# Chunk 0 of a two-layer encoder trunk: the z products of two channel groups side by side on four accumulators, with u's folds and the token rows loaded behind them

## The chip, the cores and the metric

The kernel runs on one core of a Trainium2 chip. The metric is the device time of one execution in microseconds: the median of three runs. All matrix work is done on TensorE (PE in the profile); VectorE (DVE), ScalarE (ACT) and GpSimd (POOL) convert, evict and do the elementwise work; SyncE (SP) issues nearly all transfers.

## The reference, cut to what matters

The input is x with 2048 rows (tokens) of 1024 channels. Layer 0, around which the change turns:

```python
h = rms_norm(x, a_norm)                     # per row
u, z = jnp.split(h @ a_w_in, 2, axis=-1)    # 1024 columns each
# u: four groups of 256 channels; trailing means over 2, 4, 8, 16 rows, minus the row itself
pooled = stack(means) - u
mixed = einsum('bsgc,gcd->bsgd', pooled, w_group) * scale
x = x + (mixed * silu(z)) @ a_w_out
x = x + (p @ ple_w) * sigmoid(x @ ple_gate_w)
```

Layer 1 is a stick-breaking attention of 16 heads with shared keys and values, again with a SiLU gate, an output product and the gated embedding.

## The kernel before

The 2048 rows are cut into four chunks of 512. In the first part of the kernel each chunk runs through 22 steps in a list `steps`: eight z and u steps (four groups of 256 channels each), four output products (`run_o`), four gates with embedding (`run_g`), and six for q, k and v (`run_kvq`). The attention, with what is left of layer 1 as filler, is the second part.

**Products.** Each fp32 operand is split in a high and a low half in a 'round' format that TensorE takes at one pass, and a product is three passes: high times high, high times low, low times high. So `product` for 256 output channels runs over 8 slices of 128 input channels (kt), with 2 blocks x 3 passes = 6 matmuls of 128x128 against 512 rows each: 48 matmuls, into two accumulators in PSUM. Between the slices it takes one step of a generator `beside`, with which other work is written into TensorE's program. The row norm is multiplied in only when the sums are evicted, so that products can run before the norm is known.

**Folds.** The group maps (`grp`, 256x256) are applied to u's weights instead of u: in chunk 0 `fold(g)` takes the raw weights of u (`uraw`, from `wut`), splits them (four steps `across`, ACT L418 and DVE L419), multiplies them with the map (four steps `mapped`, 12 matmuls of 256 columns each, L429, here called a fold tile) and evicts each tile in halves on ACT (L436) and DVE (L437) with the norm's gain `g_a`. Chunks 1 to 3 reread the folded weights and z's split weights from DRAM, where `queue` has stored them.

**Chunk 0's start.** `load_first(3)` queues on SP the x tiles of chunk 0 (8 of 256 KB) and the raw z weights of group 3 (4 of 256 KB) in turns. Then come fold 3's raws, its map, two small tiles of gains, fold 2's raws and its map, and, from the loop over the steps, z2's raws. `prep(0)` splits the x tiles (L326, L327); `first_weights` splits the z weights with the gain (ACT L356, DVE L360). The order of the steps is z3, u3, z2, u2, z1, u1, z0, u0. In it:

- z3 runs beside `prep`'s last steps and the `across` steps of fold 3; `first_beside` writes the fold's tiles behind it. Then come the stores of z3's split weights (`settle`) and the loads of the four token tiles (`load_tokens`, 512 KB each). z3 stays in its accumulators.
- u3 runs beside fold 2 and the squares of the tokens (ACT L306). Behind it `bcast` turns the row factor (L249: four transposes) and spreads it to the tile `rb` (L254), and `gate_of` evicts z3 (DVE L511, sigmoid on ACT L512, GpSimd L513).
- z2 runs beside the `across` steps of fold 1 (`turning(1)`), u2 beside its tiles; z1 and u1 do the same for fold 0. After each u its pooling follows (L528 to L549, DVE and GpSimd).

**Order and buffers.** The program is put in its final order by a scheduler that works with costs of its own; `keep_in_program_order` (also as `stay`) pins an instruction among the pinned ones of its engine. SP's transfers of this part are pinned. PSUM has eight banks: four in `psd`, two in `psboth`, two in `pst`. `dense()` deals `psd` and `psboth` out, two to one; `turned()` gives `pst`. `pair()` gives one of 18 split tiles, the pools `wpair` and `wboth` hold 12 pairs of weights.

Of the kernel before, what the change touches and what calls it, by code (L numbers as in the profile page):

```python
# [15 lines left out]
P = 128  # L16
D = 1024
# [18 lines left out]
def trunk_kernel(ctx, tc, x, xt, pt0, wut, cols, heads, zin, grp, aout, agate, aple,  # L36
# [69 lines left out]
    class Weights:  # L106

        def __init__(self, src, kts, c0, n, gain=None, kept=None, stay=lambda ins: ins):
            self.src, self.c0, self.n, self.gain, self.kept, self.stay = src, c0, n, gain, kept, stay
            self.kk = min(W5 // n, kts)  # L110
            self.units, self.raws = [], {}
            self.k0s = list(range(0, kts, self.kk))
# [23 lines left out]
        def convert(self, half=0):  # L136
            kk, n, gain, kept, c0 = self.kk, self.n, self.gain, self.kept, self.c0
            self.reread()
            for k0 in self.part(half):
                if (kept, c0, k0) in split_once:  # L140
                    continue
                state["u"] += 1
                pr = wp[state["u"] % 2].tile([P, 2, kk, n], F32R, tag="wpair", name="wpair")
                self.units.append(pr)
                raw = self.raws.pop(k0)
                if gain is None:
                    self.stay(A.copy(out=pr[:, 0], in_=raw))  # L147
                    state["w"] += 1
                    self.stay((G if state["w"] % 3 else V).tensor_tensor(  # L149
                        out=pr[:, 1], in0=raw, in1=f(pr[:, 0]), op=ALU.subtract))  # L150
# [69 lines left out]
    with ExitStack() as st:  # L220
# [77 lines left out]
        def prep(s):  # L298
# [24 lines left out]
            for o in range(KT):  # L323
                low = (lambda: None) if s else first_weights(o)
                pr = pair("xp")
                stay(A.copy(out=pr[:, 0], in_=xs[o]) if s or o else V.tensor_copy(out=pr[:, 0], in_=xs[o]))  # L326
                stay(V.tensor_tensor(out=pr[:, 1], in0=xs[o], in1=f(pr[:, 0]), op=ALU.subtract))  # L327
# [7 lines left out]
        wz0 = {"raw": [], "pair": []}  # L335
# [12 lines left out]
        def first_weights(o):  # L348
            q, j = o // 2, o % 2
            raw, ga = wz0["raw"][q], g_a[:, o : o + 1]  # L350
            if not j:
                state["u"] += 1
                wz0["pair"].append(wp[state["u"] % 2].tile([P, 2, 2, 256], F32R, tag="wpair", name="wpair"))
            pr = wz0["pair"][q]
# [8 lines left out]
            def store():  # L363
                d = split_once["wi", wz0["c0"], 2 * q] = dram.tile([P, 2, 2, 256], F32, name=f"wz0_{q}")
                queue(out=d, in_=f(pr))
# [5 lines left out]
        def first_beside():  # L371

            raws, wg = chunk[0]["fold"].pop(3)
            lead, folded = prep(0), fold(3, raws, wg)
            next(lead)
            next(lead)

            def behind():
                for kt in range(KT):
                    next(lead, None)  # L380
                    for _ in range((0, 0, 0, 0, 0, 1, 1, 2)[kt]):
                        next(folded, None)
                    if kt == 6:
                        maps[3].convert()
                        wg.extend(maps[3].units)
                    yield
                next(folded, None)
                maps[2].convert()
                yield from folded

            return behind()

        def load_fold(g):
# [9 lines left out]
            if g < 3:  # L403
                maps[g] = Weights(grp[g], 2, 0, 256, stay=tc.keep_in_program_order)
# [3 lines left out]
        def fold(g, raws, wg):  # L408
# [13 lines left out]
            def mapped(i):  # L422
                ps = dense()
# [38 lines left out]
        def second_beside(g):  # L462
# [4 lines left out]
            for kt in range(KT):  # L467
                if g == 2 or kt > 3:
                    next(folded, None)
                if g == 2:  # L470
                    next(chunk[0]["squares"], None)
# [12 lines left out]
        def run_z(s, g, wz):  # L484
            ck = chunk[s]
            beside = ()
            if not s and g == 3:
                beside = first_beside()
                wz = wz0["pair"]
            elif not s and g:  # L490
                beside = turning(g - 1)
            elif s and g == 3:
                beside = row(s)
            pss2 = [dense(), dense()]
            product(pss2, wz, ck["x"], (0, P), range(KT), beside, by_term=not s and g == 3)
            settle()
            if not s and g == 3:
                for q in range(4):
                    load_tokens(0, q)
                ck["z3"] = pss2  # L500
                return
            if "rb" not in ck:
                ck["rb"] = bcast(ck["r"], "x")
# [13 lines left out]
        def run_u(s, g, wu):  # L517
# [3 lines left out]
            product(pss2, wu or ck["wu"].pop(g), ck["x"], (0, P), None, second_beside(g - 1) if g and not s else ())  # L521
            if "z3" in ck:
                ck["rb"] = bcast(ck["r"], "x")
                gate_of(ck, g, ck.pop("z3"))
# [296 lines left out]
        for s in range(NSUB):  # L821
            for g in (3, 2, 1, 0):
                def load(g=g, s=s, z=0):
# [4 lines left out]
                steps.append((lambda load=load: load(z=1), lambda *w, s=s, g=g: run_z(s, g, *w)))  # L828
                steps.append((load, lambda *w, s=s, g=g: run_u(s, g, *w)))
# [38 lines left out]
        maps = {3: Weights(grp[3], 2, 0, 256, stay=tc.keep_in_program_order)}  # L868
# [8 lines left out]
        ps = dense()  # L877
        for _ in range(10):
            T.matmul(ps[:, 0:P], ident, ident, start=True, stop=True)
# [7 lines left out]
        for i, (_, run) in enumerate(steps):  # L887
# [6 lines left out]
            if i in (1, 3):  # L894
                chunk[0]["fold"][1 - i // 2] = load_fold(1 - i // 2)
# [10 lines left out]
            elif i == 1:  # L906
                join_gains(wz0["gs"])
# [498 lines left out]
```

## Time and profile before

| | |
|---|---|
| median of three runs | 2639.67 us (2639.28 to 2640.36) |
| the profiled execution | 2641.07 us, span 2639.0 us |
| PE busy | 2628.7 us (100%) |
| DVE, ACT, POOL busy | 1991.9, 1422.6, 936.2 us |
| DMA, mean over the span | 228 GB/s |
| granted TensorE clock | 1.0 |
| chunk 0's z and u products | 5.54 to 121.92 us |

Times in the profile count from the start of the span. In a list of groups or in order of time, a row has start and duration in microseconds, the engine, the line of the kernel, the operation, the tile that it writes `<-` those that it reads, shapes, and a count after x; in brackets stands how long the engine had been idle and what ended that. `PEld` is the load of a matmul's stationary operand. In a table by stretch, a row has the stretch, its length, busy time with the count of instructions, the granted clock, the mean share of time that the DMA engines were busy, and GB/s. In a list of waits a row has who waited for whom, the sum in microseconds, the times and the longest.

### The profile page before, as it was taken

To read this page: it belongs to the slowest core of one execution; us is meant where nothing else is said; L and a number is where in the kernel's file an instruction comes from. 1 tells how busy PE (TensorE), PEld (TensorE's weight loads), DVE (VectorE), ACT (ScalarE), POOL (GpSimd) and SP (SyncE) were. 2 spreads that over 40 slices of the span, in tenths; PEclk is the share of its full clock that TensorE was granted. 3 is DMA by queue.
4 is the path that set the end of the run, shared out by engine and by line. 5 is a ranking of instruction groups with operands and counts; after the bars stand their busy time and mean duration, and the time that the engine had idled before them with its cause. 6 is when DMAs were issued, how large, how long until landed. Compare 5 with 4: busy or idle time off the path is not lost.

```text
span 2639.0 us, 38535 instructions
## 1 busy us (share of the span) xinstructions
PE 2628.7 (100%) x13046; PEld 2200.8 (83%) x13046; DVE 1991.9 (75%) x2583; ACT 1422.6 (54%) x2770; POOL 936.2 (35%) x740
## 2 busy tenths in 40 slices
PE   9999999999999999999999999999999999999999
PEld 7888888888888888888888888888888888888887
DVE  6877835677367763767599999999999998886642
ACT  5456623556136641355466666666666666665530
POOL 2664437644485444744221111122111211112320
PEclk9999999999999999999999999999999999999999
DMA  8648885588856878446787665656666777779875
GB/s 327 228 166 291 307 311 186 191 285 282 308 172 228 295 247 307 148 162 231 239 279 238 185 217 168 183 168 193 209 200 181 187 222 233 201 208 288 249 231 179
DMA packets 472994, 602.26 MB, mean 228 GB/s; under 512 B 29855, under 2 KB 309663, under 8 KB 472797
## 3 DMA queue, kind: packets, MB, share of 16 engines
q1 hardware_dynamic: 466008, 588.72, 67.9%
q0 software_dynamic: 4608, 8.39, 2.0%
q10 hardware_dynamic: 2180, 2.69, 0.4%
q8 instruction: 103, 1.69, 0.3%
q14 instruction: 95, 0.77, 0.1%
HBM read 440.24 MB, written 153.17 MB: 225 GB/s over the span
## 4 chain that ended last, share of the span: by engine, by line
PE 98%; DMA 1%; DVE 0%; ACT 0%; issue 0%; POOL 0%; SPq 0%; DVEq 0%; ACTq 0%
PE psd L176 27%; PE psd L658 20%; PE psa L1023 9%; PE psd L1085 6%; PE psd L1087 6%; PE psd L1089 6%; PE pso L1036 5%; PE psl L999 5%; PE pso L1035 5%; PE psl L998 5%; PE psdt L1085 1%; PE psdt L1087 1%; PE psdt L1089 1%; PE psd L429 1%; DMA xn<-in_x_dram 0%; DMA xin<-in_xt_dram 0%
## 5 line engine op out<-in xcount | busy, mean ns | idle before, releaser
L658 PE MATMUL psd<-wpair,x 128*128 128x512 f32 x2304 | 523.9, 390 | 0.0
L1010 DVE TENSOR_TENSOR_SCAN pp<-kap,pp,zeros 128x512 f32<-128x512 f32 x384 | 513.0, 1337 | 6.4 <-ACT kap L1002 5.5
L1026 ACT CAST at<-psa 128x512 fp32r<-128x512 f32 (+3 forms) x640 | 325.2, 523 | 345.9 <-PE psa L1023 334.5
L658 PEld LDWEIGHTS psd<-wpair,x 128*128 128x128 f32 x2304 | 432.3, 188 | 89.4
L1027 DVE TENSOR_TENSOR at<-psa,at 128x512 fp32r<-128x512 f32 (+3 forms) x640 | 374.8, 597 | 62.1 <-ACT at L1026 57.9
L1002 ACT ACTIVATE kap<-psl 128x512 f32<-128x512 f32 (+3 forms) x640 | 345.7, 540 | 90.0 <-PE psl L999 86.7
L176 PE MATMUL psd<-xp,wpair 128*128 128x512 f32 x1536 | 352.7, 390 | 1.0 <-DMA wpair<-wu 0.6
L176 PEld LDWEIGHTS psd<-xp,wpair 128*128 128x128 f32 x1536 | 287.2, 188 | 61.6 <-issue 1.0
L1023 PE MATMUL psa<-ident,pp 128*128 128x128 f32 x2176 | 328.8, 273 | 0.8 <-DVE at L1027 0.8
L1023 PEld LDWEIGHTS psa<-ident,pp 128*128 128x128 f32 x2176 | 264.0, 141 | 54.8 <-DVE at L1027 2.3
L998 PE MATMUL psl<-kk,qa 128*128 128x512 f32 (+3 forms) x640 | 275.4, 430 | 0.0
L1007 DVE TENSOR_TENSOR_SCAN pp<-kap,ahead 128x128 f32<-128x128 f32 (+3 forms) x256 | 226.0, 885 | 37.1 <-ACT kap L1002 35.7
L1036 PE MATMUL pso<-at,vv 128*128 128x512 f32 (+3 forms) x640 | 234.2, 366 | 0.0
L999 PE MATMUL psl<-kk,qb 128*128 128x512 f32 (+3 forms) x640 | 233.1, 364 | 0.0
L1035 PE MATMUL pso<-at,vv 128*128 128x512 f32 (+3 forms) x640 | 232.3, 363 | 0.0
L155 DVE SCALAR_TENSOR_TENSOR wpair<-wraw,gains,wpair 128x512 fp32r<-128x512 f32 x192 | 167.2, 891 | 58.2 <-ACT wpair L154 53.2
L176 PE MATMUL psd<-x,wpair 128*128 128x512 f32 x768 | 176.7, 389 | 0.0
L176 PE MATMUL psd<-mp,wpair 128*128 128x512 f32 x768 | 174.7, 389 | 0.0
L149 POOL TENSOR_TENSOR wpair<-wraw,wpair 128x512 fp32r<-128x512 f32 x99 | 144.1, 1464 | 76.7 <-ACT wpair L147 69.3
L176 PEld LDWEIGHTS psd<-x,wpair 128*128 128x128 f32 x768 | 144.2, 188 | 29.8
L176 PEld LDWEIGHTS psd<-mp,wpair 128*128 128x128 f32 x768 | 144.2, 188 | 29.9
L154 ACT ACTIVATE wpair<-wraw,gains 128x512 fp32r<-128x512 f32 x192 | 131.7, 717 | 59.5 <-DMA wraw<-in_bq_dram 30.0
(191 smaller groups left out, 4454.9 us busy)
## 6 DMA issues: line engine op xcount, KB each, us to landing
kk<-kd SPq DMA_DIRECT2D x160, 256.0 KB
vv<-vd SPq DMA_DIRECT2D x160, 256.0 KB
wraw<-in_kv_dram SPq DMA_DIRECT2D x128, 256.0 KB
wpair<-wzd SPq DMA_DIRECT2D x64, 512.0 KB
wpair<-wod SPq DMA_DIRECT2D x64, 512.0 KB
wpair<-wgd SPq DMA_DIRECT2D x64, 512.0 KB
wpair<-wu SPq DMA_DIRECT2D x48, 512.0 KB
wpair<-wi SPq DMA_DIRECT2D x36, 512.0 KB
```

What stands on the lines that cost most here:

```text
L176: T.matmul(ps, wst(units, kt, wh, c0), acts[kt][:, ah], start=(first and not wh and not ah), stop=(last and wh == 1))
L658: T.matmul(pss2[i], ck["x2"][kt][:, xh, tk], wst(ws, kt, wh, 0, W5), start=(kt == 0 and xh == 0 and wh == 0), stop=(kt == KT - 1 and wh == 1))
L998: T.matmul(ps[:, :w], qa[:, qs], kk[:, :w], start=True, stop=False)
L999: T.matmul(ps[:, :w], qb[:, qs], kk[:, :w], start=False, stop=True)
L1002: A.activation(out=kp[:, r0:], in_=ps[:, :w], func=AF.Sigmoid, scale=-1.0)
L1007: V.tensor_tensor_scan(out=pp[:, r0:][:, ::-1], data0=kp[:, r0:][:, ::-1], data1=ahead[:, r0:][:, ::-1], initial=1.0, op0=ALU.mult, op1=AL ...
L1010: V.tensor_tensor_scan(out=pp[:, ::-1], data0=kp[:, ::-1], data1=zeros.to_broadcast([P, W5]), initial=st["carry"][j], op0=ALU.mult, op1=AL ...
L1023: T.transpose(pt[:, j * P : (j + 1) * P], pp[:, r0 + kt * P : r0 + (kt + 1) * P], ident)
L1026: A.copy(out=at[:, 0, cs], in_=pt[:, cs])
L1027: V.tensor_tensor(out=at[:, 1, cs], in0=pt[:, cs], in1=f(at[:, 0, cs]), op=ALU.subtract)
L1035: T.matmul(po[:, cs], vv[:, kt, :], at[:, 0, cs], start=(st["diag"] and kt == 0), stop=False)
L1036: T.matmul(po[:, cs], vv[:, kt, :], at[:, 1, cs], start=False, stop=(st["last"] and kt == 3))
```

## The change

The first two steps of chunk 0 become one, `run_first`: z3 and z2 run quarter by quarter (two x tiles, then six matmuls a tile for group 3, and the same for group 2) on four accumulators, which take all of `psd`. `load_first` queues the raw weights of both groups between the x tiles; group 2's raws lie in the pool `tmp`. The token tiles are queued behind fold 3's raws and the gains, ahead of fold 2's raws; the stores of the split z weights (now eight) come behind all of these. The squares run within `run_first`, behind the last `across` steps of fold 3; then come one tile of fold 3, `bcast`, the gates of z3 and z2, fold 2's map, and the other three tiles. Fold 3's tiles use `psboth` and `pst`; the warm-up matmuls use `pst`. The maps' split pairs come from `pair()`. The steps then are u3 (beside fold 2), u2 (beside fold 1's `across`), z1 (beside its tiles), u1 (beside fold 0's `across`), z0 (beside its tiles), u0. `load_fold(1)` and `load_fold(0)` are queued ahead of u3 and u2.

```diff
-                state["u"] += 1
-                pr = wp[state["u"] % 2].tile([P, 2, kk, n], F32R, tag="wpair", name="wpair")
+                if self.home:
+                    pr = self.home("gmap").rearrange("q e (k n) -> q e k n", n=n)
+                else:
+                    state["u"] += 1
+                    pr = wp[state["u"] % 2].tile([P, 2, kk, n], F32R, tag="wpair", name="wpair")
...
             for o in range(KT):
-                low = (lambda: None) if s else first_weights(o)
+                low = (lambda: None) if s else first_weights(3, o)
...
+                if not s and o % 2:
+                    first_weights(2, o - 1)()
+                    first_weights(2, o)()
...
-        def load_first(g):
-
-            wz0["c0"] = D + g * 256
+        def load_first():
+
             tc.keep_in_program_order(nc.scalar.dma_start(out=g_a, in_=cols[:, 0:KT]))
             for q in range(4):
-                raw = (wraw if q < 3 else io).tile([P, 2, 256], F32, tag="wraw" if q < 3 else "io", name="wraw")
-                wz0["raw"].append(raw)
-                if q:
+                raw3 = (wraw if q < 3 else io).tile([P, 2, 256], F32, tag="wraw" if q < 3 else "io", name="wraw")
+                raw2 = tmp("wraw").rearrange("q (k n) -> q k n", k=2)
+                wz0[3]["raw"].append(raw3)
+                wz0[2]["raw"].append(raw2)
+                for k, (g, raw) in enumerate(((3, raw3), (2, raw2))):
+                    xin = io.tile([P, W5], F32, tag="io", name="xin")
+                    o = 2 * q + k
+                    queue(out=xin, in_=xt[o * P : (o + 1) * P, 0:W5])
                     queue(out=raw, in_=zin[4 + g, q])
-                load_x(0, q, lambda: queue(out=raw, in_=zin[4 + g, 0]))
...
+                    chunk[0].setdefault("xs", []).append(xin)
...
+        def run_first():
+
+            ck = chunk[0]
+            raws, wg = ck["fold"].pop(3)
             lead, folded = prep(0), fold(3, raws, wg)
...
+            accs = {g: [psd.tile([P, W5], F32, tag="psd", name="psd") for _ in range(2)] for g in (3, 2)}
+            for _ in range(4):
+                next(lead)
+            for q in range(4):
+                for g in (3, 2):
+                    for kt in (2 * q, 2 * q + 1):
+                        for wh, ah in ((0, 0), (0, 1), (1, 0)):
+                            for k, ps in enumerate(accs[g]):
+                                T.matmul(ps, wst(wz0[g]["pair"], kt, wh, k * P), ck["x"][kt][:, ah],
+                                         start=(kt == 0 and not wh and not ah), stop=(kt == KT - 1 and wh == 1))
+                next(lead, None)
+                next(lead, None)
+                if q == 1:
+                    next(folded)
+                    next(folded)
+                elif q == 2:
+                    maps[3].convert()
+                    wg.extend(maps[3].units)
+                    next(folded)
+                    next(folded)
+                    next(ck["squares"])
+                    next(ck["squares"])
+            for _ in ck["squares"]:
+                pass
+            settle()
+            next(folded)
+            ck["rb"] = bcast(ck["r"], "x")
+            for g in (3, 2):
+                gate_of(ck, g, accs[g])
+            maps[2].convert()
+            for _ in folded:
+                pass
...
             def mapped(i):
-                ps = dense()
+                if g < 3:
+                    ps = dense()
+                elif i % 2:
+                    ps = turned().rearrange("q j t -> q (j t)")
+                else:
+                    ps = psboth.tile([P, W5], F32, tag="psd", name="psd")
...
-            product(pss2, wu or ck["wu"].pop(g), ck["x"], (0, P), None, second_beside(g - 1) if g and not s else ())
-            if "z3" in ck:
-                ck["rb"] = bcast(ck["r"], "x")
-                gate_of(ck, g, ck.pop("z3"))
+            beside = ()
+            if not s:
+                beside = {3: lambda: second_beside(2), 2: lambda: turning(1), 1: lambda: turning(0), 0: tuple}[g]()
+            product(pss2, wu or ck["wu"].pop(g), ck["x"], (0, P), None, beside)
...
+            if not s:
+                steps.append((lambda: (None,), lambda w: run_first()))
+                steps.append((lambda: (None,), lambda w: None))
+            for z, g in ((1, 3), (0, 3), (1, 2), (0, 2), (1, 1), (0, 1), (1, 0), (0, 0)) if s else (
+                    (0, 3), (0, 2), (1, 1), (0, 1), (1, 0), (0, 0)):
...
-        load_first(3)
+        load_first()
         chunk[0]["fold"][3] = load_fold(3)
         maps[3].fetch()
-        wz0["gs"] = load_gains()
+        given = load_gains()
+        for q in range(4):
+            load_tokens(0, q)
         chunk[0]["fold"][2] = load_fold(2)
...
-        ps = dense()
+        ps = turned()
         for _ in range(10):
-            T.matmul(ps[:, 0:P], ident, ident, start=True, stop=True)
+            T.matmul(ps[:, 0], ident, ident, start=True, stop=True)
...
-            if i in (1, 3):
-                chunk[0]["fold"][1 - i // 2] = load_fold(1 - i // 2)
+            if i in (2, 3):
+                chunk[0]["fold"][3 - i] = load_fold(3 - i)
```

More of the change, by code (lines that the diff above doesn't have):

```diff
@@ L106, in trunk_kernel, with __init__ @@
     class Weights:
-        def __init__(self, src, kts, c0, n, gain=None, kept=None, stay=lambda ins: ins):
+        def __init__(self, src, kts, c0, n, gain=None, kept=None, stay=lambda ins: ins, home=None):
             self.src, self.c0, self.n, self.gain, self.kept, self.stay = src, c0, n, gain, kept, stay
+            self.home = home
             self.kk = min(W5 // n, kts)
@@ L334, in prep, with first_weights @@
                 yield
[L335 to L339 removed]
+        wz0 = {g: {"raw": [], "pair": []} for g in (3, 2)}
+        def load_first():
             tc.keep_in_program_order(nc.scalar.dma_start(out=g_a, in_=cols[:, 0:KT]))
             for q in range(4):
[L342 to L344 removed]
+                raw3 = (wraw if q < 3 else io).tile([P, 2, 256], F32, tag="wraw" if q < 3 else "io", name="wraw")
[6 more added lines that the diff above has]
+                    queue(out=xin, in_=xt[o * P : (o + 1) * P, 0:W5])
                     queue(out=raw, in_=zin[4 + g, q])
[L346 to L348 removed]
+                    chunk[0].setdefault("xs", []).append(xin)
+        def first_weights(g, o):
             q, j = o // 2, o % 2
[L350 removed]
+            raw, ga = wz0[g]["raw"][q], g_a[:, o : o + 1]
             if not j:
                 state["u"] += 1
[L353 to L354 removed]
+                wz0[g]["pair"].append(wp[state["u"] % 2].tile([P, 2, 2, 256], F32R, tag="wpair", name="wpair"))
+            pr = wz0[g]["pair"][q]
             tc.keep_in_program_order(
@@ L369, in first_weights @@
             return low
-        def first_beside():
-            raws, wg = chunk[0]["fold"].pop(3)
+        def run_first():
+            ck = chunk[0]
+            raws, wg = ck["fold"].pop(3)
             lead, folded = prep(0), fold(3, raws, wg)
[L375 to L391, printed above, removed]
+            accs = {g: [psd.tile([P, W5], F32, tag="psd", name="psd") for _ in range(2)] for g in (3, 2)}
[30 more added lines that the diff above has]
+                pass
         def load_fold(g):
@@ L403, in load_fold @@
             if g < 3:
-                maps[g] = Weights(grp[g], 2, 0, 256, stay=tc.keep_in_program_order)
+                maps[g] = Weights(grp[g], 2, 0, 256, stay=tc.keep_in_program_order, home=pair)
                 maps[g].fetch()
@@ L469, in second_beside @@
                     next(folded, None)
-                if g == 2:
-                    next(chunk[0]["squares"], None)
                 yield
@@ L486, in run_z @@
             beside = ()
[L487 to L492, printed above, removed]
+            if not s:
+                beside = second_beside(g)
+            elif g == 3:
                 beside = row(s)
             pss2 = [dense(), dense()]
-            product(pss2, wz, ck["x"], (0, P), range(KT), beside, by_term=not s and g == 3)
+            product(pss2, wz, ck["x"], (0, P), range(KT), beside)
             settle()
[L497 to L502, printed above, removed]
-                ck["rb"] = bcast(ck["r"], "x")
             gate_of(ck, g, pss2)
@@ L821, in trunk_kernel, with load @@
         for s in range(NSUB):
-            for g in (3, 2, 1, 0):
-                def load(g=g, s=s, z=0):
+            if not s:
+                steps.append((lambda: (None,), lambda w: run_first()))
+                steps.append((lambda: (None,), lambda w: None))
+            for z, g in ((1, 3), (0, 3), (1, 2), (0, 2), (1, 1), (0, 1), (1, 0), (0, 0)) if s else (
+                    (0, 3), (0, 2), (1, 1), (0, 1), (1, 0), (0, 0)):
+                def load(g=g, s=s, z=z):
                     if not s and not z:
@@ L827, in load @@
                     return (Weights(zin, KT, z * D + g * 256, 256, g_a, "wi"),)
-                steps.append((lambda load=load: load(z=1), lambda *w, s=s, g=g: run_z(s, g, *w)))
-                steps.append((load, lambda *w, s=s, g=g: run_u(s, g, *w)))
+                steps.append((load, lambda *w, s=s, g=g, run=run_z if z else run_u: run(s, g, *w)))
             for b in range(4):
```

7 lines of the change are left out of this document (3 added, 4 removed).

## The prediction

> **What bounds the kernel now.** I read the page's first table, then the list of waits with TensorE as the waiting engine, then busy time by stretch, because an average of 100% can hide the few microseconds that an edit of one stage can reach.
>
> ```profile
> PE 2628.7 (100%) x13046; PEld 2200.8 (83%) x13046; DVE 1991.9 (75%) x2583; ACT 1422.6 (54%) x2770; POOL 936.2 (35%) x740
> ```
> ```profile
> PE psd L879 <- POOL ident masks.py:199: 1.4, 1, 1.4
> PE psd L429 <- ACT wt L418: 1.1, 1, 1.1
> PE psd L429 <- POOL wpair L149: 1.0, 1, 1.0
> PE psd L429 <- ACT wpair L147: 0.8, 1, 0.8
> PE psa L1023 <- DVE at L1027: 0.8, 3, 0.3
> PE psd L176 <- DMA wpair<-wu: 0.6, 1, 0.6
> PE psd L176 <- ACT xp L326: 0.3, 1, 0.3
> PE psd L429 <- DVE wt L419: 0.2, 1, 0.2
> ```
> TensorE sets the time, and its waits (total, times, longest, in us) are few. Four at line 429 and the one for `xp` lie in the stretch that the diff rewrites, chunk 0's start: 3.4 us. The warm-up wait (1.4), the `wpair<-wu` wait (chunk 3) and the attention part (L1023) aren't touched. So the change can win a few microseconds of 2640 at most, and the sum has to be made in tenths.
>
> A listed wait is not all that is lost: a matmul that waits briefly counts as busy. I therefore price the work at its undisturbed rate, from the chain of waits, and compare it with the clock time of each stretch.
>
> ```profile
> 65.36 1.43 PE psd L429 x12
> ...
> 100.30 119.71 PE psd L176 x528
> ```
> ```profile
> 42.82 0.44 PE pst L249 x4
> ```
> ```profile
> core 0: us, PE busy (x), PEclk, DMA share, GB/s
> 5.54:18.44 12.90, 11.77 (x49) 1.00 0.97 342
> 18.44:25.53 7.09, 6.12 (x48) 1.00 0.94 332
> 25.53:47.51 21.98, 20.68 (x115) 1.00 1.03 410
> 47.51:121.92 74.41, 74.41 (x373) 1.00 0.70 252
> ```
> A 512-column matmul takes 119.71/528 = 0.2267 us and a fold tile of 12 matmuls takes 1.43. Eight products of 48 (chunk 0's z and u) are 384 x 0.2267 = 87.05 us, 16 fold tiles 22.9, the four transposes of `bcast` 0.44: 110.4 us of work in the 116.4 of the four rows, so **6.0 us are lost**. By stretch: z of group 3 (48 x 0.2267 = 10.9 of 12.9) loses 2.0, fold 3 (5.7 of 7.1) 1.4, u3 with fold 2 (48 matmuls of u3 and the first 13 of z2: 61 x 0.2267 + 5.7 + 0.4 = 20.0 of 22.0) 2.0, all later ones together (275 x 0.2267 + 11.4 = 73.8 of 74.4) 0.6.
>
> **The change part by part.** The profiled execution took 2641.07 us for a span of 2639.0, 1.40 us above the median of 2639.67; I form a difference of spans and take it from the median.
>
> *Loads.* Now x tiles and z3's raws (12 of 256 KB), fold 3's (4 + 1), two small ones, fold 2's (4 + 1), z2's raws (4), z3's stores (4 of 512 KB), then tokens (4 of 512 KB). After: x, z3's and z2's raws (16), fold 3 (4 + 1), the small ones, tokens (8 units of 256 KB), fold 2 (5), then eight stores (16 units). The tokens pass fold 2, z2's raws and the stores on SP's queue; fold 2 falls behind the tokens; the first store falls from the 27th unit to the 35th.
>
> ```profile
> 4.76 6.65 DMA xin<-in_xt_dram
> ...
> 11.43 6.32 DMA wraw<-in_grp_dram
> ...
> 23.06 9.21 DMA xn<-in_x_dram
> ```
> The ninth transfer landed at 4.76 + 6.65 = 11.41, the seventeenth at 17.75: 6.34/8 = 0.79 us for each 256 KB. The rule holds further on: the first token is the 36th unit now, which gives 17.75 + 19 x 0.79 = 32.8, and it landed at 32.27. After the change the last x tile or raw (16th unit) lands near 17.0, fold 3's map (21st) 20.9, the last token (29th) 27.2, fold 2's map (34th) 31.2, the last store (50th) 43.8.
>
> *z3 and z2 together.* The loads of the first product's first matmul keep their places, so the start stays at 5.54. A quarter (two x tiles, both groups) is 24 matmuls, 5.4 us of TensorE, fed by 4 transfers (3.2 us), by ScalarE and by VectorE.
>
> ```profile
> 5.79 0.60 ACT L326 CAST xp<-xin 128x512 fp32r<-128x512 f32 x1
> 6.43 0.69 DVE L327 TENSOR_TENSOR xp<-xin,xp 128x512 fp32r<-128x512 f32 x1 [0.43 <-ACT xp L326]
> 6.53 0.51 ACT L356 ACTIVATE wpair<-wraw,g_a 128x256 fp32r<-128x256 f32 x1
> 7.04 0.48 DVE L360 SCALAR_TENSOR_TENSOR wpair<-wraw,g_a,wpair 128x256 fp32r<-128x256 f32 x1
> ```
> ScalarE needs 2 x (0.60 + 0.51 + 0.51) = 3.2 us a quarter and VectorE 2 x (0.69 + 0.48 + 0.48) = 3.3. Today a quarter is only 2.7 us of TensorE against 3 transfers (2.4), which is why it stumbles 2.0 us here. After, only z2's first raw (4th transfer, near 11.41 - 5 x 0.79 = 7.5, plus 0.5 for its ScalarE pass) is due about when it arrives (5.54 + 12 x 0.2267 = 8.3). The z2 passes are moved, not added (8 on each of the two engines). I bound the loss from below by 0 and from above by today's 2.0, and take 0.5, nearer 0, as every feeder needs 60% of TensorE's time. End of both products: 5.54 + 96 x 0.2267 + 0.5 = 27.8.
>
> *Fold 3.* Its map lands at 20.9 and the four `across` steps lie before 23, so the 0.8 and 1.0 us waits of fold 3 go: cover 4.6 us. Its four tiles go to `psboth` and `pst`, two buffers each, since the four `psd` buffers hold the sums; no tile waits for an eviction.
>
> *Tokens, norm and `bcast`.* What is late next is the norm. It was consumed behind u3; now its transposes stand in TensorE's program behind the first of four fold tiles, and three tiles and u3 queue behind them.
>
> ```profile
> 36.97 1.06 ACT L306 ACTIVATE xn<-xn 128x1024 f32<-128x1024 f32 x1
> 37.93 0.18 ACT L306 ACTIVATION_READ_ACCUMULATOR xn<-xn 128x1 f32 x1
> ...
> 38.48 1.04 POOL L87 TENSOR_TENSOR rx<-ms,neghalf 128x4 f32<-128x4 f32 x1
> ...
> 43.29 0.59 ACT L254 COPY rbx<-pst 128x512 f32<-128x512 f32 x1 [2.37 <-PE pst L249]
> 43.91 0.69 DVE L511 TENSOR_TENSOR zr<-psd,rbx 128x512 f32<-128x512 f32 x1 [2.47 <-ACT rbx L254]
> ```
> From the last token to the norm: 38.11 - 36.97 = 1.2 on ScalarE (the other squares lie before) and 39.52 - 38.11 = 1.4 on GpSimd, so 27.2 + 2.6 = 29.8. TensorE is through the first tile at 27.8 + 1.4 = 29.2: **a new wait of 0.6**. Its bounds: 0 if the instruction scheduler puts a second tile ahead, 1.6 if the tokens are a microsecond later. I take 0.6, which the load rate gives. Then `rb` is ready near 31.0, the four z evictions of 0.69 follow, and u3's two buffers are free at 32.4, while the three tiles keep TensorE until 29.8 + 0.4 + 4.3 = 34.5: covered by 2.1. If that cover were gone, each microsecond would cost one.
>
> *Fold 2, stores, next weights.* Fold 2's map conversion (31.2) stands on ScalarE ahead of fold 3's evictions 2 to 4; a tile takes two passes of 0.44 on VectorE (two in 0.87, row below) and two on ScalarE in turn, some 1.7 us, so the tiles are ready at 33.5, 35.2 and 36.9, and u3 asks for them at 34.5 + 2.7, 5.4 and 8.2: covered by 3.7. Fold 2's own waits of 1.1 and 0.2 came from `across` steps that ScalarE ran between the late squares; both are earlier now, and go. Its tiles take weight buffers of z3 and z2, whose stores land from about 32.8 on, 1.6 us each, against a first need at 34.5 + 5 x 1.36 + 1.4 = 42.7. z1's raws come behind fold 1 (59th unit, near 51) for z1 at 61: a cover of 10. The maps' buffers, the warm-up's other PSUM buffer and the store order cost nothing I can find.
>
> *Order of the steps.* u2 now follows u3 at once, and u1 follows z1; a fold's tiles lie beside the product just ahead of the one that uses them. A tile has from its own end 8.2 us (3 more steps of 2.8, or u2's first six steps).
>
> ```profile
> 52.19 0.87 DVE L437 SCALAR_TENSOR_TENSOR wpair<-psd,g_a,wpair 128x256 fp32r<-128x256 f32 x2
> ...
> 53.88 1.63 DVE L549 SCALAR_TENSOR_TENSOR po<-po,gains,zr 128x512 f32<-128x512 f32 x1
> 55.44 0.47 DVE L437 SCALAR_TENSOR_TENSOR wpair<-psd,g_a,wpair 128x256 fp32r<-128x256 f32 x1
> ...
> 60.27 0.74 DVE L549 SCALAR_TENSOR_TENSOR po<-po,gains,zr 128x512 f32<-128x512 f32 x1
> ```
> Fold 2's last tile left TensorE at 47.7, as the row of later stretches begins, and was whole at 55.91: 8.2 us, with the z gate and u3's pooling on VectorE at once. After the change the z gate is out of the way by then, so I take 0 here and keep up to 2 as a rival. The 0.6 us of the later stretches I leave.
>
> *Sum.* Lost before 6.0; after 0.5 + 0.6 + 0.6 = 1.7. Gain 4.3: 2639.67 - 4.3 = **2635.4 us**, 0.16% faster. A measurement of this kernel can tell about 0.2% (5.3 us) from no change, so that is "within 0.2%".
>
> **Two rules of the Trainium skill beside it.** The row gave 0.79 us per 256 KB, or 332 GB/s, and a last token at 27.2. The Trainium skill's page "DMA: Bandwidth & Descriptors", Specifications, puts the limit of HBM for one core at about 358 GB/s; an estimate by that is 0.73 us a transfer, a last token at 26.5, no wait at the `bcast`, and 2634.8. The two rows of L549 above show one operation at 0.74 and at 1.63 us. The Trainium skill's page "SBUF — State Buffer", Who interferes with whom, says that a VectorE operation with two SBUF inputs contends with a GpSimd operation that reads SBUF; that speaks against four gates on GpSimd beside u3's start, though by the same rule the z evictions, with one input in PSUM, stay free, and their rows (0.69) agree.
>
> **The rivals.**
> - *The norm is in time.* If the scheduler places the transposes later, as it did before (the transposes ran before fold 2's last tile, which the program has ahead of them), or loads run at the 410 GB/s of a later row, the 0.6 goes; without the 0.5 too, and with the 0.6 us wait for `wpair<-wu` in chunk 3 shifted away, 2639.67 - 6.0 + 0.6 - 0.6 = 2633.7. Against it: every small loss must go at once. Chance 0.20, and in three of four of these past 0.2%.
> - *Fold tiles late at u2 or u1.* Today's 8.2 us is just the time there is, and the first of the two passes at 52.19 ends the tile before it, which left TensorE at 42.8, ahead of the transposes in the row above: 10 us, 2 too many. One such wait gives 2637.4, two 2639.4. For it: u3's pooling meets u2 directly. Against: at 43 to 46 the gate's four operations were in the same queue. Chance 0.14.
> - *Nothing gained*: the first product runs at the pace of its loads as now (2.0), and `bcast` waits 1.6: 0.6 + 2.0 + 1.6 = 4.2 lost, plus one late tile of 2.0: 2639.9. Chance 0.06.
> - *Slower: the tokens.* All of TensorE's program after the first fold tile now stands behind the last token, one for one. Before, a token took 9.2 us from issue to landing, and 36 units were ahead. At a wait of 0.6 + 4.3 = 4.9, a last token at 31.5, the kernel is as it was; at 36.8 it is 0.2% slower; were they to land behind the eight stores and fold 2 (50th unit, 43.8), the wait would be 17.2 and the time 2652. Against: SP's queue is kept in program order, and 29 units are ahead. Chance 0.08, 0.07 of it beyond 0.2%.
>
> **How the numbers follow.** The forecast (2634.4 to 2637.0, from 0 or 1.6 at the `bcast`) has 0.52. Range 2633.8 to 2639.6: it leaves out the slower rival, nothing gained, and the edge of the first rival. Faster by over 0.2%: 0.15; slower by over 0.2%: 0.07; within: 0.78.
>
> **What would show it.** Right: the three waits of line 429 for L147, L149 and L418 gone; the first 96 matmuls end near 27.8; one wait of under 2 us at line 249's transposes near 29; u3 from about 34.5; chunk 0's output products starting near 117.6 (121.9 now). Wrong: a wait of several microseconds at line 249, or ahead of u2's fifth or seventh step for a fold tile (L437), or x tiles that pace the first products.

## The result and the profile after

The changed kernel took 2660.03 us (median of six runs, 2658.36 to 2660.67) against 2640.02 (six runs, 2638.98 to 2641.67): a ratio of 1.0075, 95% interval 1.0062 to 1.0088. It is **20 us slower**, where 4.3 us of gain was forecast. The profiled execution took 2659.84 us for a span of 2658.1, 19.1 us above the span of before. Of all the executions behind this document one stands far apart: 9410.22 us, in the first kernel of experiment 6, whose other ten lie between 2637.53 and 2642.08; the ratio given there leaves it out.

The first table and the list of TensorE's waits of the changed kernel (columns as before):

```profile
PE 2636.2 (99%) x13046; PEld 2201.6 (83%) x13046; DVE 1984.3 (75%) x2583; ACT 1418.4 (53%) x2770; POOL 932.7 (35%) x740
```
```profile
PE psd L180 <- DVE x L263: 4.5, 5, 1.2
PE psd L180 <- DVE wpair L469: 3.6, 1, 3.6
PE psd L180 <- ACT x L262: 3.0, 3, 1.5
PE psd L180 <- DMA wpair<-wu: 2.0, 2, 1.2
PE psd L678 <- DVE x L272: 1.6, 3, 0.6
```

The four waits of the fold tiles are gone, as forecast. New are one wait of u1 for the eviction of a fold tile (L469, 3.6 us in one piece) and many small ones for `x`, the input of the gates: neither stood in the list of before. The wait for `wpair<-wu` grew from 0.6 to 2.0. `x` is made by the output products of every chunk, so most of the loss lies far behind the lines that the diff touches. TensorE in order of time and by stretch shows chunk 0 itself:

```profile
5.31 22.09 PE L395 MATMUL psd<-xp,wpair 128*128 128x512 f32 x96
27.24 1.59 PE L461 MATMUL psd<-gmap,wt 128*128 128x256 f32 x12
28.67 0.60 PE L253 MATMUL pst<-ident,rx 128*128 128x128 f32 x4
33.41 6.99 PE L180 MATMUL psd<-xp,wpair 128*128 128x512 f32 x30
...
76.30 1.59 PE L461 MATMUL psd<-gmap,wt 128*128 128x256 f32 x12
81.54 20.45 PE L180 MATMUL psd<-xp,wpair 128*128 128x512 f32 x78 [3.65 <-DVE wpair L469]
```
```profile
5.31:27.24 21.93, 21.93 (x100) 1.00 1.02 357
27.24:33.41 6.17, 6.17 (x54) 1.00 1.03 418
33.41:50.13 16.72, 16.72 (x99) 1.00 1.04 406
50.13:77.73 27.60, 27.60 (x146) 1.00 0.59 222
77.73:122.62 44.89, 41.24 (x194) 0.92 0.61 223
```

From 5.31 to 77.73 there is no wait. The work in it, at the prediction's undisturbed rates, is five products (240 x 0.2267 = 54.4), twelve fold tiles (17.2) and the transposes (0.44): 72.0 us in 72.4. So this part loses 0.4. The old order lost 6.0 over all eight products, 5.4 of it before 47.51. Behind 77.73 come the 3.65 us at u1's first matmul, and 78 matmuls that take 20.45 us instead of 78 x 0.2267 = 17.7. The granted clock says why, in a finer table by stretch:

```profile
75.00:82.00 7.00, 3.35 (x20) 0.86 0.19 75
82.00:85.00 3.00, 3.00 (x8) 0.50 0.75 302
85.00:90.00 5.00, 5.00 (x19) 0.81 0.47 186
```

After the wait the clock was at half for the whole 3 us row, in which 8 matmul records stand; that costs another 2.8 us. So chunk 0's output products begin at 122.62: 0.7 later than before, where 3.65 + 2.8 of loss less 5.6 us of gain should give 0.8, and a start that is 0.2 earlier 0.6.

The other 18.3 us come later. Set beside the starts of the same matmuls of before, the kernel falls back in chunk 0 by 2.6 us at the change from output products to gates and 2.0 at q; in chunk 1 by 1.1, 1.3 and 4.1; in chunk 2 by 4.5 at the gates and 0.8 at q; in chunk 3 by 0.6 and 1.1; at the end of the first part it is 18.8 us late, at its last matmul 19.0. The list's waits for `x` are only 9.1 us of this. Part of the rest is that a matmul which stands alone between two waits takes 0.51 us (175.57 in the rows below), where one in a chain takes 0.2267, and that the clock fell once more (0.72 from 498 to 504 us, in chunk 1's first gate). What the queue of loads waits for around the first of these places, SP's list of waits, after (119 to 180 us), then before (118 to 180):

```profile
SPq L96 <- POOL wpair L153: 37.0, 6, 17.2
```
```profile
SPq L96 <- DVE wpair L149: 25.6, 5, 8.9
SPq L96 <- POOL wpair L149: 9.0, 7, 3.1
```

L153 (L149 before) makes the low half of a split weight. Before, SP waited mainly for low halves that VectorE makes; after, for low halves that GpSimd makes, up to 17.2 us at a time. What follows from it, in order of time on SP, ScalarE, VectorE and TensorE, after:

```profile
126.42 19.00 SPq L96 DMA_DIRECT2D wraw<-in_agate_dram  x4
...
146.94 14.24 SPq L96 DMA_DIRECT2D wraw<-in_agate_dram  x4
...
161.75 0.38 SPq L96 DMA_DIRECT2D kraw<-in_bgate_dram  x1
...
166.56 0.62 ACT L262 CAST kpair<-kraw 128x512 fp32r<-128x512 f32 x1 [8.64 <-DMA kraw<-in_bgate_dram]
...
167.73 1.37 DVE L153 TENSOR_TENSOR wpair<-wraw,wpair 128x512 fp32r<-128x512 f32 x1 [8.05 <-ACT wpair L151]
...
174.90 1.22 ACT L262 CAST x<-ta 128x512 fp32r<-128x512 f32 x2 [1.34 <-DVE ta L604]
...
175.57 0.51 PE L180 MATMUL psd<-x,wpair 128*128 128x512 f32 x1 [0.76 <-ACT x L262]
177.24 2.79 PE L180 MATMUL psd<-x,wpair 128*128 128x512 f32 x11 [1.17 <-DVE x L263]
```

Twice four issues of weights stretch over 19.0 and 14.24 us, and the `kraw` load behind them is issued at 161.75. (The `kraw` tiles are raw weights for the second part of the kernel, which it splits and stores on the way.) ScalarE stands 8.64 us at the conversion of this `kraw`, which has not landed, and VectorE 8.05 us for the half of a weight that ScalarE makes next. Both are behind with their work from there on: the sum that VectorE makes from the output product (`ta`, L604) and the split of `x` behind it come late, and TensorE waits.

**Which counter did it.** In the code, every raw weight that is fetched through `fetch` takes the next value of `state["raw"]`: each third goes to the pool `wraw` (three buffers), the others to `io` (ten). Every low half of L153 (the group maps and the output, gate and embedding weights, which carry no gain) takes the next value of `state["w"]`: each third goes to VectorE, the others to GpSimd. Before, z2's four raws were fetched through the same function; the change loads them apart, so `raw` is 4 lower from then on, a shift of one step modulo 3. Of the weights split at L153, those in the small pool were the ones whose low half VectorE makes; after, they are ones of GpSimd, and SP, whose transfers are pinned in program order, stands until the buffer is free. Each later chunk takes 84 raws and 36 such halves, both multiples of three, and so keeps this phase. Two more counters lose calls by the change, the one that deals weight pairs to two pools (four calls) and the one in `dense()` (nine calls, period three). Those are whole periods, so behind chunk 0's z and u steps both stand as before.

### The profile page after: what moved, and what is told of

Same layout as the page of the kernel before. It is cut to its first block, busy times and chain, and to the rows that moved or that the text cites. A ratio compares the mean times of both kernels' runs of the same rounds, so it can differ in the third digit from the quotient of the medians.

```text
span 2658.1 us, 38468 instructions
## 1 busy us (share of the span) xinstructions
PE 2636.2 (99%) x13046; PEld 2201.6 (83%) x13046; DVE 1984.3 (75%) x2583; ACT 1418.4 (53%) x2770; POOL 932.7 (35%) x740
## 4 chain that ended last, share of the span: by engine, by line
PE 56%; DVE 0%; issue 0%; ACT 0%; DMA 0%; SPq 0%; DVEq 0%; ACTq 0%
PE psa L1048 9%; PE psd L1110 6%; PE psd L1112 6%; PE psd L1114 6%; PE psd L678 5%; PE pso L1061 5%; PE psl L1024 5%; PE pso L1060 5%; PE psl L1023 5%; PE psd L180 2%; PE psdt L1110 1%; PE psdt L1112 1%; PE psdt L1114 1%; DMA wraw<-in_agate_dram 0%; SPq L96 0%
## 5 line engine op out<-in xcount | busy, mean ns | idle before, releaser
L180 PE MATMUL psd<-xp,wpair 128*128 128x512 f32 x1440 | 332.4, 391 | 5.7 <-DVE wpair L469 3.6
L180 PEld LDWEIGHTS psd<-xp,wpair 128*128 128x128 f32 x1440 | 271.1, 189 | 62.6 <-DVE wpair L469 3.9
L1147 POOL TENSOR_TENSOR zr<-zr,sgz 128x512 f32<-128x512 f32 x32 | 62.5, 1953 | 259.8 <-ACT sgz L1146 242.1
```

Source lines behind the costliest of these rows:

```text
L180: T.matmul(ps, wst(units, kt, wh, c0), acts[kt][:, ah], start=(first and not wh and not ah), stop=(last and wh == 1))
```

## Experiments

In the expectations, A is this phase of the two counters, B that lateness is merely handed on, C the queue of u2's pooling ahead of u1's fold tiles, E the clock, G the PSUM buffers of those tiles. The other rivals are named there. Medians are of ten or eleven runs where nothing else is said. The kernel before, measured beside them, took 2639.57 us (beside the kernels of 1 and 3), 2639.29 (of 2, 4 and the shorter filler of 5) and 2639.16 us (the longer filler and 6); ratios, with their 95% intervals, are to these executions and lie up to 0.04% beside the quotient of the medians.

**1. The phase, put back and put in.** One line in the loop over the steps, ahead of any of the later fetches. To the changed kernel:

```diff
         for i, (_, run) in enumerate(steps):
+            if i == 5:
+                state["raw"] += 1
```

> The changed kernel with one line more: ahead of chunk 0's last z and u steps the counter that deals weight raws out to the pools (two of three to io, one of three to wraw) goes up by one, so that from the output products on every raw lies in the same pool as in the kernel before. Theory A (the change left that counter at another phase, and SP's queue waits for raws whose reader on GpSimd comes late): the losses behind chunk 0's z and u steps, 18.3 us up to the attention, go, while the 3.65 us wait at u1 stays: about 2642 us, and no wait of TensorE at the first gate product of a chunk. Theory B (lateness handed on: chunk 0's output weights are queued late behind stores of late fold tiles): the counter is irrelevant, 2660 us, with the same waits.

Measured: 2642.85 us, 1.0009 [1.0000, 1.0019]; 17.2 us of the 20 are back. Its list of TensorE's waits has the fold tile and one wait for reread weights (in chunk 2), and none for `x`:

```profile
PE psd L180 <- DVE wpair L469: 3.7, 1, 3.7
PE psd L180 <- DMA wpair<-wu: 1.5, 1, 1.5
```

SP (118 to 182 us) waits as in the kernel before, mostly for VectorE and 9.8 us at most:

```profile
SPq L96 <- DVE wpair L153: 22.3, 4, 9.8
SPq L96 <- POOL wpair L153: 5.6, 4, 3.1
```

The same place of the kernel before, nothing else touched, shifted to the phase of the changed kernel:

```diff
+            if i == 5:
+                state["raw"] += 2
```

> The kernel before with the same counter raised by two at that place, so that its raws lie as in the changed kernel from the output products on; its chunk 0 start is untouched. Theory A: 10 to 18 us slower than the kernel before (2650 to 2658), with waits of TensorE for the split of x at the first gate product of each chunk. Theory B: 2640 us, no such waits.

Measured: 2656.27 us (four runs), 1.0061 [1.0046, 1.0076]; SP's waits and TensorE's are like those of the changed kernel, in the program that knows nothing of the new start:

```profile
SPq L96 <- POOL wpair L149: 41.6, 6, 17.3
```
```profile
PE psd L176 <- DVE x L259: 5.1, 6, 1.2
PE psd L176 <- ACT x L258: 3.5, 5, 0.8
```

One line of bookkeeping costs 16.7 us here and gives back 17.2 there. That is the larger loss, shown from both sides.

**2. The same alignment by the other counter, and the third phase.** To the changed kernel, instead:

```diff
+            if i == 5:
+                state["w"] += 2
```

> The changed kernel with, at the same place as in the first experiment, not the counter of raws but the counter that picks the engine of the low half (VectorE for every third, GpSimd for the others) raised by two. Both have period three. Theory A1 (what matters is their alignment: with the change, the raws in the small pool wraw, three buffers, are those whose low half GpSimd makes, before it was VectorE; GpSimd's late reads hold the buffer for which SP's queue stands): the alignment is that of the kernel before, and the time is that of the first experiment, 2640 to 2645. Rival A2 (it is the layout of the raws over the pools as such, or the order of the instructions that follows from it): the layout is that of the changed kernel, and the time 2655 to 2660.

Measured: 2644.84 us, 1.0022 [1.0013, 1.0031]; 15.2 of the 20 us are back by changing only who splits what. Set beside the starts of before, it loses nothing in chunks 1 to 3, where the changed kernel loses 13.3. SP's waits in chunk 1, changed kernel (440 to 508 us) and this one (440 to 506):

```profile
SPq L96 <- POOL wpair L153: 45.7, 6, 17.3
```
```profile
SPq L96 <- DVE wpair L153: 29.1, 6, 8.2
```

In chunk 0, though, it loses 2.4 and 2.2 us, about as much as the changed kernel (2.6 and 2.0), and SP's wait there is 40.6 us with VectorE as the releaser. Experiment 1 has neither. So in chunk 0 it also counts which of the loads fall in the small pool, not only which engine frees them; that part isn't taken apart further.

The third phase of the counter of raws, in the changed kernel:

```diff
+            if i == 5:
+                state["raw"] += 2
```

> The changed kernel with the counter of raws raised by two, the third of the three phases; GpSimd makes the low half of every raw in wraw here too. A1: slow like the changed kernel, 2652 to 2662, with SP's queue waiting for GpSimd's reads of raws. A2: no forecast better than between 2640 and 2660; a time near 2642 would speak against A1.

Measured: 2685.02 us (four runs), 1.0174 [1.0160, 1.0188]: the direction expected, the size not. Of the three phases one is harmless, one costs 17 us and one 42. TensorE's main wait is again the split of `x`, in longer pieces:

```profile
PE psd L180 <- ACT x L262: 23.2, 4, 7.8
```

SP's list around the first gates (37.0 us for GpSimd, 13.9 at the longest) looks no worse than the changed kernel's, so why this phase costs 25 us more than that one isn't shown.

**3. The wait at u1.** VectorE in order of time before u1, changed kernel:

```profile
75.30 1.77 DVE L563 SCALAR_TENSOR_TENSOR po<-work 128x512 f32<-128x512 f32 x1 [2.10 <-POOL work L559]
77.40 0.75 DVE L569 SCALAR_TENSOR_TENSOR po<-po,gains,zr 128x512 f32<-128x512 f32 x1
78.07 0.48 DVE L469 SCALAR_TENSOR_TENSOR wpair<-psd,g_a,wpair 128x256 fp32r<-128x256 f32 x1
...
81.00 0.88 DVE L469 SCALAR_TENSOR_TENSOR wpair<-psd,g_a,wpair 128x256 fp32r<-128x256 f32 x2 [0.54 <-ACT wpair L468]
```

u2's pooling waits for GpSimd's sums and stands ahead of fold 1's evictions. To take GpSimd out of it, in the changed kernel:

```diff
-                    (G if sh in (2, 4) else V).tensor_tensor(
+                    (G if sh in (2, 4) and (s or g != 2) else V).tensor_tensor(
```

> The changed kernel with the two middle shifted adds of u2's pooling in chunk 0 on VectorE instead of GpSimd, so that VectorE, which has fold 1's evictions behind that pooling in its queue, waits for GpSimd no more there. Theory C (fold 1's first tile is late at u1 because its eviction stands behind the pooling, and the wait of 3.65 us halves TensorE's clock for a few us after): the pooling ends 2 to 3.5 us sooner, the wait at u1 falls below 1.5 us, the clock stays at 1.0 between 82 and 90 us, and the whole is 4 to 6 us faster than the changed kernel if the later losses stay: 2654 to 2656. Rival D (the tile is late by TensorE's own order or by its weight buffer): the wait stays at 3 to 4 us and the time at 2660. Theory B, if right as well, would let the chunk 0 part of the later losses (5 us) go too.

Measured: 2657.19 us (four runs), 1.0064 [1.0049, 1.0079]. The wait went from 3.65 to 1.97, not below 1.5; the clock stayed whole (1.00 from 75 to 90 us), so the matmuls behind it lost nothing more (17.98 us for 78), and the output products began at 118.48 instead of 122.62. The losses of the phase stay, as they should, and are larger by 2 us in this run: of the 4.1 us gained at the output products 2.0 are left at the end of the first part. The whole is 2.8 us faster than the changed kernel, where 4 to 6 were expected.

```profile
79.86 17.98 PE L180 MATMUL psd<-xp,wpair 128*128 128x512 f32 x78 [1.97 <-DVE wpair L469]
```

This together with the phase put back (the edit of experiment 1):

> Both edits, the counter's phase of the kernel before and u2's pooling on VectorE. Theories A and C together: both losses go and the gain of chunk 0's start is left, about 2635 us, 4 to 5 us faster than the kernel before. If A is wrong: 2654. If C is wrong: 2642.

Measured: 2638.95 us, 0.9995 [0.9986, 1.0004], 4 us above the figure expected; the same 1.97 us wait, and output products from 118.47.

**4. Another order of the same work.** The phase put back, and u2's pooling written behind z1's product, with its first addition pinned there:

```diff
+            if "pool" in ck:
+                ck.pop("pool")()
             settle()
             gate_of(ck, g, pss2)
...
-            for k in range(2):
-                ...
+            def pool():
+                for k in range(2):
+                    ...
+                        if not s and g == 2 and not k and sh == 1:
+                            tc.keep_in_program_order(ins)
...
+            if not s and g == 2:
+                ck["pool"] = pool
+            else:
+                pool()
```

> The first experiment (counter restored) with u2's pooling in chunk 0 written behind z1's product and its first add pinned on VectorE behind fold 1's evictions; engines as in the changed kernel. Theory C: the evictions run as each tile is done, u1 doesn't wait, the clock stays at 1.0, and chunk 0's output products begin 6.5 us earlier than in the first experiment, near 117 us; 2635 to 2637, 3 to 5 us faster than the kernel before. If another wait takes its place (u2's pooling late for the buffer that u1's eviction writes): the wait moves to a later product and the time is 2638 to 2643.

Measured: 2642.62 us, 1.0012 [1.0003, 1.0021]: the wait at u1 is gone and the clock stays whole there, but VectorE now comes late to the evictions of z1 (0.8 us of wait at z0) and of z0 (2.5 us at u0):

```profile
PE psd L180 <- DVE zr L533: 3.3, 2, 2.5
```

A wait moved, not removed.

**5. The clock apart from the wait.** The phase put back, and matmuls of the identity (128 columns, result unused) written ahead of u1, 8 and then 17 of them (16 and 34 records):

```diff
             if not s and g == 1:
+                ps = turned()
+                for _ in range(8):     # 17 in the second
+                    T.matmul(ps[:, 0], ident, ident, start=True, stop=True)
```

> The first experiment (counter restored) with eight identity matmuls of 128 columns ahead of u1's product, which read nothing that is late; they write a PSUM tile that nobody reads. In the warm-up such a matmul took 0.41 us, so they fill 3.3 of the 3.66 us in which TensorE waited for fold 1's tile. Theory E (the wait itself lets the granted clock drop to one half for some us, which costs 3 us more): the clock stays at 1.0, the 78 matmuls from u1 on take 17.7 to 18.0 us instead of 20.8, and the whole takes 2640, 3 us less than the first experiment. Rival F (these matmuls are slow because later tiles of fold 1 come late one by one): 20.8 us and 2643 as before.

Measured: 2640.73 us, 1.0006 [0.9997, 1.0015]. The eight took 1.95 us, not 3.3, and left a wait of 1.87, and the 78 matmuls took 19.58 us. By stretch the clock still falls, less deep:

```profile
82.00:85.00 3.00, 2.54 (x7) 0.66 0.65 262
```

> As the run with eight identity matmuls ahead of u1, with seventeen. There eight took 1.95 us and left a wait of 1.87; seventeen take 4.1 us and end with fold 1's tile or 0.5 us after it. Theory E (the clock falls because TensorE stands still): granted clock 1.0 from 75 to 90 us, the 78 matmuls from u1 on in 17.7 to 18.0 us (20.8 without filler, 19.6 with eight), and about 2639.5 to 2641. Rival F: 19.5 us or more all the same.

Measured: 2640.24 us, 1.0001 [0.9992, 1.0010]. The filler fills the whole gap, u1 starts hardly earlier (82.07; 82.29 in experiment 1), and yet the 78 matmuls take 17.97 us where they took 20.83 in experiment 1:

```profile
78.26 3.96 PE L543 MATMUL pst<-ident 128*128 128x128 f32 x34
82.07 17.97 PE L180 MATMUL psd<-xp,wpair 128*128 128x512 f32 x78
```
```profile
82.00:85.00 3.00, 3.00 (x15) 1.00 0.65 259
```

From 85 to 90 us the clock is 1.00 too. So 2.9 us of the loss at u1 (20.83 - 17.97) are the clock, brought on by the idle time and not by slower operands. In time it is 2.6 us (2642.85 to 2640.24), or 2.2 when each is set against the kernel before beside it. The Trainium skill's page "TensorE: Matmul & The Clock Gate", Why this matters for your kernels, warns of idle gaps of TensorE above about 3 us; the 3.65 us gap here agrees. The 1.87 us behind the eight identity matmuls are less than that and brought the clock down all the same, while 1.97 us left it whole in experiment 3; these runs don't explain it.

**6. What u1 waits for.** The list names the eviction of a fold tile (L469), and as weights u1 takes fold 1's tiles one after the other, slice by slice. But its first matmul also needs an empty accumulator, and the one that `dense()` deals to it is that of fold 1's second tile, whose last half leaves with the first of the two at 81.00 above, at 81.48; u1 begins at 81.54. The phase put back, and fold 1's tiles in other banks:

```diff
-                if g < 3:
+                if g == 1:
+                    state["d"] += 1
+                    ps = turned().rearrange("q j t -> q (j t)") if i % 2 else psd.tile([P, W5], F32, tag="psd", name="psd")
+                elif g < 3:
                     ps = dense()
```

> The first experiment (counter restored) with fold 1's four tiles of chunk 0 in psd and pst in turns instead of the buffers that dense() deals out; the count of dense() goes on as it did, so u1's two sums get psboth and psd as before, but the buffers there are not those of fold 1's tiles; the order on VectorE stays. Theory G (what u1's first matmul waits for is the buffer in PSUM that fold 1's second tile holds until VectorE has evicted it, at the fourth of the eight halves, 81.5 us in the changed kernel): u1 begins when its first tile's high half is there, within 1 us of its turn (78 us), the clock stays at 1.0, output products of chunk 0 begin near 117.5, and the whole takes 2635 to 2638. Theory C as first put (fold 1's first tile is late as weight of u1): no change of buffers helps, the wait stays above 1.5 us and the time at 2641 to 2643.

Measured: 2638.66 us, 0.9998 [0.9989, 1.0007], 0.7 us above the range expected. u1 begins at 77.80, straight behind the tiles:

```profile
77.80 0.63 PE L180 MATMUL psd<-xp,wpair 128*128 128x512 f32 x2
78.67 17.53 PE L180 MATMUL psd<-xp,wpair 128*128 128x512 f32 x76 [0.24 <-DVE wpair L472]
```

The weight that it does need is late by 0.24 us; the other 3.4 were the buffer. The evictions on VectorE are as late as before, the second tile's last half among them:

```profile
81.07 0.48 DVE L472 SCALAR_TENSOR_TENSOR wpair<-pst,g_a,wpair 128x256 fp32r<-128x256 f32 x1 [0.54 <-ACT wpair L471]
```

so their lateness alone was not what cost u1 its start. TensorE now arrives at the output products at 117.31 and meets new waits behind it: 1.3 us for `mp` (L263) among these products, and 0.7 in all for `wpair<-wu` in chunks 1 and 3. With u2's pooling on VectorE as well (experiment 3):

> The run with both edits (counter restored, u2's pooling on VectorE) with fold 1's tiles in psd and pst as well. G: its last wait at u1 (1.97 us) goes too, and the whole takes 2635 to 2637, 3 to 5 us less than the kernel before; no faster than the run without the pooling on VectorE by more than 1 us. C: 2638 to 2640 as without.

Measured: **2635.73 us, 0.9985 [0.9976, 0.9994]**, faster than the changed kernel and, by 0.15% (0.13% by the medians), than the one before. That is less than the 0.2% which the prediction took as its limit, but with these 11 runs the interval leaves out 1. Its whole list of TensorE's waits:

```profile
PE pst L907 <- POOL ident masks.py:199: 1.4, 1, 1.4
PE psa L1053 <- DVE at L1057: 0.8, 3, 0.3
```
```profile
116.34 13.99 PE L180 MATMUL psd<-mp,wpair 128*128 128x512 f32 x61
```

It is 2.9 us better than the kernel ahead of it, where at most 1 was expected: the 1.3 and 0.7 us are gone as well. The output products begin 5.58 us earlier than before. Of this the medians show 3.4 us (2639.16 to 2635.73) and the two profiled spans 6.0 (2639.0 to 2633.0); before's profiled execution lay 1.9 us above this median and the other 0.9 below its own, and where those differences arise no view shows.

## Why the prediction was wrong

The mechanism for the rewritten stretch held. The failure is in two sentences that priced what lies behind it at nothing.

- *z3 and z2 together*: end at 27.24, forecast 27.8. They began 0.2 earlier, and of the loss of 0.5 there was 0.2 (21.93 against 96 x 0.2267 = 21.76).
- *Tokens, norm and `bcast`*: the wait of 0.6 didn't come. The last token's square and the norm, in order of time:

```profile
25.15 1.06 ACT L310 ACTIVATE xn<-xn 128x1024 f32<-128x1024 f32 x1
...
26.68 1.04 POOL L87 TENSOR_TENSOR rx<-ms,neghalf 128x4 f32<-128x4 f32 x1
```

The norm was ready at 27.72, not 29.8: the last token was there by 25.15, not 27.2, since the transfers went faster than the 332 GB/s that I took from the old start. From 8 to 16 us, with loads alone, they went at 393 GB/s, and at 357 on average over the whole stretch. Why the old start was slower no run here shows. A later row of before has 410 GB/s; the prediction named it in the rival of the norm in time, and that rival had this part right. By the 358 GB/s of the Trainium skill's page "DMA: Bandwidth & Descriptors", Specifications, the prediction had an estimate of 26.5 for the token and no wait. No wait came, but the trace's rates lie above that figure: the 393, and the 418 and 406 of the next two rows. The slower rival, late tokens, did not happen.
- *Fold 3, fold 2, stores*: right, no wait to 77.73. u3 from 33.41 (34.5 forecast).
- *Order of the steps*, "I take 0 here and keep up to 2 as a rival": **the term was mis-sized and its releaser misread.** One place was late, as in the rival of late fold tiles, but by 3.65 us, and with the clock 6.2 to 6.5, where the rival had 2. I measured how long a tile may take until it is wanted as a weight; the first thing wanted was the PSUM bank in which it lay. `dense()` deals `psboth` to folds and to u's sums alike, and with u1 right behind its four tiles, whose evictions on VectorE stood behind u2's pooling, the bank came back late. Without that the kernel gains what the sum said. No wait of before exceeded 1.4 us, so the clock had no term; a rival that allows a wait should have asked what it does to the clock.
- *"The maps' buffers, the warm-up's other PSUM buffer and the store order cost nothing I can find"*, and no term behind chunk 0: **the step that failed by the most.** I followed the moved loads as transfers through SP's queue and never as calls to a function with a counter. Skipping four calls to it changed, from chunk 0's output weights to the end of the first part, which engine frees the small pool: 17 us. Nothing in the profile of before shows the counter; its two rows of SP's waits (VectorE's and GpSimd's low halves, 25.6 and 9.0 us) would have shown that SP already stood waiting for buffers of raw weights.

With both put right (experiment 6) the time is 2635.73 us; the sum of the prediction was 2635.4. That it is so close is in part chance: the start gains 5.6 where 4.3 was forecast, the median shows 3.4 of it, and this kernel has other banks for fold 1 and another engine for u2's pooling than the kernel that was forecast.

## What to carry to other kernels

When an edit bypasses a helper that deals buffers or engines by a running counter, everything dealt afterwards shifts: list each counter that the removed or added calls advance, modulo its period, before calling the rest of the program unchanged. A wait that the profile puts down to an eviction may be for the bank and not for the value; ask what the first waiting instruction writes as well as what it reads. And price a wait on the main engine with what the clock loses behind it.

## What the runs showed of the hardware

One idle time of 3.65 us on TensorE (changed kernel) brought the granted clock to 0.50 in the 3 us row behind it, 0.86 and 0.81 in the rows on both sides, and cost 2.5 to 2.9 us more than the wait itself. An idle time of 1.97 us behind a fold tile's matmuls (experiment 3) left the clock at 1.00. One of 1.87 us behind 1.95 us of short identity matmuls brought it to 0.66, and 3.96 us of these in place of the wait kept it at 1.00 (experiment 5). Waits of 0.75 and 1.16 us with one matmul between them went with a clock of 0.72 in chunk 1 of the changed kernel (498 to 504 us), while 0.76 and 1.17 us in chunk 0 left it at 1.00 (175 to 180 us); what decides between these no run shows. The DMA engines moved 393 GB/s with loads alone (8 to 16 us, changed kernel) and 406 to 418 over 17 and 6 us where stores were queued as well.
